# Five weight pieces of the mixing product split during the product before it, and one low part moved from GpSimd to VectorE

## The chip, the cores and the metric

The kernel runs on one core of a Trainium2 chip. The metric is the device time of one execution in microseconds (us). TensorE (PE) does the matrix products, VectorE (DVE) and ScalarE (ACT) the elementwise work, GpSimd (POOL) some of it too, and SyncE (SP) issues most of the DMAs that bring weights in.

## The reference, cut to what matters

The kernel computes one hybrid decoder block on x of 512 tokens by 1024 channels in float32:

```python
h = rmsnorm(x, norm1_g)
z = h @ w_in + b_in                     # split into glu, rx, rg, ga, gb
u = silu(layernorm(causal_conv(glu)))
y_a = u @ conv_w_out + conv_b_out       # "ya" in the kernel
y_b = (rg_lru(...) * gelu(rg)) @ lru_w_out
m = sigmoid(ga) * y_a + sigmoid(gb) * y_b
x = x + m @ w_mix_out                   # "mixing" (mx) in the kernel
h = rmsnorm(x, norm2_g)
x = x + (silu(h @ w1) * (h @ w3)) @ w2
return rmsnorm(x, norm_f_g)
```

## The kernel before, in words

Every matrix product in float32 is made of three products of split operands: each operand is cut into a high part, which ScalarE casts (`act.copy`, L128), and a low part, which is the rest (`sub`, L124), made by VectorE or by GpSimd. TensorE multiplies high by high, high by low and low by high.

The work runs in stages, in this order: z (in-projection), the convolution and the recurrence beside it, yb (L652), ya (`ya_group`, matmuls at L1393), mixing (`m7`, a `Sevenfold`, matmuls at L1316), the second norm with its transposes (`turn_half`, "th", L697) and the feed-forward layer (fr at L1567, then or). The products of ya and of mixing are done with seven block products in place of eight, so that some of their weights are sums of blocks: b11, b21, b22 are blocks of the weight matrix, and t1 to t4 are sums, which DMAs on GpSimd's queue add up in DRAM beforehand (tiles cot1 to cot4 and mxt1 to mxt4). ya is done in two groups, each with seven pieces (b11, b21, b22, t2, t1, t3, t4); 24 matmuls read each piece. Each piece of mixing's weights holds two blocks of 128x512.

All weights stream through one list of pieces ("chunks"). `wchunk` appends a piece to the list; SP's loads, ScalarE's casts and the low parts follow the order of that list. A piece is loaded into one of RAW = 8 raw tiles of 128x1024 (0.5 MB, tiles `raw_...`); a raw tile is free again when the low part of the piece eight places ahead of it has been made. The split goes either to one of HL = 5 tiles with room for both parts (`where="hl"`, tiles `hl_...`), which is free again when TensorE has read it; or, with `where="long"`, to four tiles of 128x512 from the pool of long-lived tiles: then it takes two casts and two subtractions of 128x512 in place of one each of 128x1024. `weights(key, ahead)` is what a product calls for its piece: it emits the splits up to `ahead` places beyond it. Before the change mixing's pieces stand behind all of ya's in the list, and all of them go to `hl` tiles.

Of mixing's pieces one, t4_0, has its low part made by GpSimd (`on_pool`), and one, b22_2, has its low part put off (`put_off`, done by `lows_put_off`). Then `mix_end` does the end of mixing: `second` is the last of the products with t2 and b22, `less` and `plus` subtract PSUM banks from, and add them to, the residual tiles x200 to x231 (x2, token tile t, half h), `scaled` and `scale` multiply by the reciprocal of the norm (tiles xs, L1469), `third` does the products with t4, and `turn_half` the transposes, whose outputs VectorE turns into h20l to h27l (L701). The feed-forward products start with fr<-h20h.

VectorE, ScalarE and SP take their instructions strictly in order. In the profile the tile names lack their digits: hl_cot is any of the pieces t1 to t4 of ya, hl_cob any of b11, b21, b22 of ya; hl_mxb and hl_mxt the same for mixing; mxr is any bank of mixing's products.

Of the kernel before, what the change touches and what calls it, by code (L numbers as in the profile page):

```python
# [8 lines left out]
F32 = mybir.dt.float32  # L9
# [4 lines left out]
P = 128  # L14
T = 512
# [11 lines left out]
ND = D // P  # L27
# [30 lines left out]
SUMS_OWN = 40  # L58
LO_BY_DVE = 8
MID_AT, MID_STEP = 38, 2  # L60


MIX_LATE_LAG, LATE_LAG = 1, 8
# [23 lines left out]
def tile_block(ctx, tc, a, out):  # L87
# [24 lines left out]
    vec, act, pe, pool_e = nc.vector, nc.scalar, nc.tensor, nc.gpsimd  # L112
# [5 lines left out]
    newest = {}  # L118
    put_off = []
# [3 lines left out]
    def sub(eng, o, x, y):  # L123
        return eng.tensor_tensor(out=o, in0=x, in1=y, op=ALU.subtract)  # L124

    def split_to(h, l, full, eng, copy=act.copy):

        newest["cast"] = copy(h, full)  # L128
        if eng is None:
            put_off.append((l, full, h.bitcast(F32)))  # L130
            return h, l
        last = sub(eng, l, full, h.bitcast(F32))
        newest["sub" if eng is pool_e else "low"] = last.ins
        return h, l

# [26 lines left out]
    def wchunk(key, src, kt, cols, where="hl", lo=pool_e, after=None):  # L162
        chunks.append((key, src, kt, cols, where, lo, after))
# [49 lines left out]
    def weights(key, ahead=AHEAD):  # L213
        i = next(i for i, c in enumerate(chunks) if c[0] == key)
        emit_to(i + 1 + ahead)
        newest["at"] = i
        return held.pop(key)
# [57 lines left out]
    def co_quarter(n, g):  # L275

        if n[0] == "t":
            assert "co" in sums_made
            return co_sums[n][:, g]
        k = CO_PAIRS[g][int(n[2]) - 1]  # L280
        c = 4 * (int(n[1]) - 1)
        return conv_out[:, c : c + 4, 2 * k * P : 2 * (k + 1) * P]

    CO_ORDER = [(n, g) for of in (("b11", "b21"), ("b22", "t2", "t1", "t3", "t4")) for g in range(2) for n in of]

    def co_chunk(n, g):

        def load(raw_t):
            newest["load"] = newest["any"] = nc.sync.dma_start(raw_t.rearrange("p (k n) -> p k n", k=4), co_quarter(n, g)).ins

        wchunk(f"co{n}_{g}", load, 4, 2 * P, lo=vec)

    for n, g in CO_ORDER:
        co_chunk(n, g)

    class Quartered:
        def __init__(self, name, w, kh, lo, parts=(), step=None, on_pool=(), put_off=()):


            self.name, self.w, self.kh = name, w, kh  # L300
            self.step = step or 1
            self.tile = lambda k, i: k + kh * i if self.step == 1 else 2 * k + i
            self.parts = {n: [None] * kh for n in parts}

            self.all_sums = {n: dram.tile([P, kh, T], F32, tag=f"{name}{n}", name=f"{name}{n}") for n in IN_PLACE if n not in parts}
            self.sums = {(n, k): v[:, k, :] for n, v in self.all_sums.items() for k in range(kh)}
            self.at = {}

            def quarter(n, k):
                if n[0] == "t":  # L310
                    assert self.name in sums_made
                    return self.sums[n, k]
                i, h = int(n[1]) - 1, int(n[2]) - 1
                return w[:, self.tile(k, i), h * T : (h + 1) * T]

            def chunk(key, of):
                def load(raw_t):
                    for i, q in enumerate(of):
                        nc.sync.dma_start(raw_t[:, i * T : (i + 1) * T], quarter(*q))

                for i, q in enumerate(of):
                    self.at[q] = (f"{name}{key}", i)
                wchunk(f"{name}{key}", load, len(of), T, lo=None if key in put_off else pool_e if key in on_pool else lo)


            for p_ in (("b11", "t1", "b21"), ("t2", "t3", "b22"), ("t4",)):
                p_ = [n for n in p_ if n not in parts]
                for k in range(kh):
                    if len(p_) % 2 and k % 2 == 0:
                        chunk(f"{p_[-1]}_{k}", [(p_[-1], i) for i in (k, k + 1) if i < kh])  # L330
                    if len(p_) > 1:
                        chunk(f"{p_[0]}_{k}", [(n, k) for n in p_[:2]])

        def order(self):
            return [self.tile(k, i) for k in range(self.kh) for i in range(2)]

        def get(self, k, *names, ahead=AHEAD):

            out = []
            for n in names:  # L340
                if n in self.parts:
                    out.append(self.parts[n][k])
                    continue
                key, i = self.at[n, k]
                if key not in self.loaded:
                    self.loaded[key] = weights(key, ahead)
                h, l = self.loaded[key]
                out.append((h[:, i, :], l[:, i, :]))
            return out

        loaded = {}

    mixq = Quartered("mx", a["w_mix_out"][0].rearrange("(k p) n -> p k n", p=P), ND // 2, vec, step=2, on_pool=("t4_0",), put_off=("b22_2",))
    w1 = a["ffn_w1"][0].rearrange("(k p) n -> p k n", p=P)
    w3 = a["ffn_w3"][0].rearrange("(k p) n -> p k n", p=P)

# [15 lines left out]
    def f_both(n, k, lo=vec):  # L372

        def load(raw_t):
            for i, w_ in enumerate((w1, w3)):
                if n[0] == "b":
                    src = f_quarter(n, k, w_, 0, 4)
                else:
                    c, e, _ = WHERE[n]
                    src = f_sums[k][:, i, int(c[1]), :].rearrange("p (k n) -> p k n", k=4)[:, :, e * P : (e + 1) * P]  # L380
                newest["any"] = nc.sync.dma_start(raw_t[:, i * T : (i + 1) * T].rearrange("p (k n) -> p k n", k=4), src).ins

        wchunk(f"f{n}_{k}", load, 8, P, lo=lo)
# [155 lines left out]
    for k in range(KF):  # L539
# [6 lines left out]
        else:  # L546
# [3 lines left out]
            if k + 1 in SEVEN:  # L550
                for j in BEGUN_LATER:
                    for n in ("b11", "b21", "t4"):
                        f_both(n, j)
    outq = Quartered("o", a["ffn_w2"][0].rearrange("(k p) n -> p k n", p=P), NF // 2, vec, step=2, on_pool=("t4_6",))
    x2_kept = [[dram.tile([P, T], F32, tag=f"x2k{t}{h}", name=f"x2k{t}{h}") for h in range(2)] for t in range(NT)]


# [105 lines left out]
    def rstd_mean(ss):  # L663
        vec.tensor_scalar(out=ss[:, 0:1], in0=ss[:, 0:1], scalar1=1.0 / D, scalar2=EPS, op0=ALU.mult, op1=ALU.add)
# [798 lines left out]
    def mix_end(second, plus, less, r1, r2, r7, third):  # L1463
        sc = [[longt(f"xs{t}{h}") for h in range(2)] for t in range(NT)]
        xs.extend(sc)
        begun = [rstd_begin(x2[t][0], sc[t][0], False) for t in range(2)]

        def scale(t, i, r):
            newest["scaled"] = vec.tensor_scalar(out=sc[t][i], in0=x2[t][i], scalar1=r, scalar2=None, op0=ALU.mult).ins  # L1469

        def scaled(t, h, some=(0, 1)):
            r = rstd_end(begun[t], x2[t][h], sc[t][h])
            for i in range(2):
                if i in some:
                    scale(t, i, r)
                nc.sync.dma_start(x2_kept[t][i][:, :], x2[t][i])
            return r


        with tc.manual_schedule(engines={ET.PE, ET.Activation, ET.DVE}):  # L1480
            second()
            less(0, 1, r1[0])
            plus(0, 1, r2[0])
            less(2, 1, r1[0])
            rstd_mean(begun[0][0])
            less(1, 1, r1[1])
            plus(1, 1, r2[1])
            rstd_mean(begun[1][0])
            less(3, 1, r1[1])

            rs = [scaled(t, 1, (0,)) for t in range(2)]
            for t in range(2):
                scale(t, 1, rs[t])

            for i in range(2):
                third(i, range(2))
            for q in range(2):
                turn_half("th", xs, "norm2_g", h2p, 0, [bank, bank2], range(4 * q, 4 * q + 4))
                for i in range(2):
                    third(i, [2 + q])  # L1500


            for c in range(ND):
                f_full.append(longt(f"hf{c}"))
                full(f_full[c][:, LO], c, LO)
            for i in range(2):
                less(2 + i, 1, r7[i])
                plus(2 + i, 0, r7[i])
            begun.extend(rstd_begin(x2[t][1], sc[t][1]) for t in (2, 3))
            emit_to(emitted[0] + 1)  # L1510
            for i in range(2):
                plus(2 + i, 0, r1[i])
            for t in (2, 3):
                scaled(t, 0)
# [81 lines left out]
    class Seven:  # L1596
# [14 lines left out]
        def copy(self):  # L1611
            self.c11 = shortt(f"c11_{self.k}")
            left_over(act.copy(self.c11, self.r1).ins)
# [248 lines left out]
```

## Time and profile before

| | |
|---|---|
| median of 3 runs | 786.73 us (786.65 to 786.78) |
| the profiled execution, its own time | 786.88 us |
| its span, first to last instruction | 785.1 us |
| TensorE busy | 775.5 us (99%) |
| VectorE busy | 677.2 us (86%) |
| ScalarE busy | 489.6 us (62%) |
| GpSimd busy | 292.4 us (37%) |
| granted TensorE clock | 1.0 |
| ya's matmuls | 364.81 to 405.13 us of the span |
| mixing's matmuls | 405.13 to 449.27 us, where the feed-forward layer starts |

Times of the trace are counted from the start of the span; the execution's own time is 1.78 us longer than the span. In the trace's rows stand the start, the duration and the instruction as out<-in with its shape; `[1.85 <-DVE stats L664]` says that the engine stood idle for 1.85 us before it and what ended that. Successive instructions of one engine overlap by a little, so what an instruction takes of the engine is the distance to the next start, not its duration.

### The profile page before, as it was taken

What the parts mean: (1) busy time and instruction counts of PE and PEld (TensorE: products, weight loads), DVE (VectorE), ACT (ScalarE), POOL (GpSimd) and SP (SyncE); (2) the same over time, 40 slices, a digit from 0 to 9 for tenths busy, and PEclk for the clock granted to TensorE, in tenths of its full rate; (3) what the DMA queues carried; (4) which work ended last, traced back from release to release, by engine and by line L of the source; (5) the groups of instructions that cost most, each with busy time, mean ns of one, the idle gap of its engine ahead of it and who ended that gap; (6) DMA issues with size and microseconds to landing.
All of it is one profiled execution on the core that took longest, in us unless ns stands there. A gap on an engine that the chain in (4) does not pass through costs nothing.

```text
span 785.1 us, 12621 instructions
## 1 busy us (share of the span) xinstructions
PE 775.5 (99%) x4469; PEld 684.1 (87%) x4469; DVE 677.2 (86%) x1028; ACT 489.6 (62%) x734; POOL 292.4 (37%) x240
## 2 busy tenths in 40 slices
PE   9999999999999999999999899999999999999997
PEld 9988788888888888888998698999999999888886
DVE  6389998899987997798799969779888889999957
ACT  8543678976786777566556576455554555666844
POOL 4365856577677973311101581312212220000001
PEclk9999999999999999999999999999999999999999
DMA  8827978796999996499977676998989794679522
GB/s 246 233 58 198 261 207 241 183 275 178 260 251 285 303 284 189 104 269 294 258 253 224 185 250 213 237 290 216 268 229 245 251 215 134 220 234 299 171 68 107
DMA packets 184753, 174.39 MB, mean 222 GB/s; under 512 B 14683, under 2 KB 145907, under 8 KB 184691
## 3 DMA queue, kind: packets, MB, share of 16 engines
q1 hardware_dynamic: 166034, 131.39, 57.0%
q0 software_dynamic: 18496, 41.95, 22.8%
q8 instruction: 35, 0.57, 0.3%
q10 hardware_dynamic: 160, 0.27, 0.1%
q14 instruction: 28, 0.22, 0.1%
HBM read 149.97 MB, written 50.33 MB: 255 GB/s over the span
## 4 chain that ended last, share of the span: by engine, by line
PE 89%; DVE 7%; DMA 2%; issue 1%; ACT 0%; SPq 0%; DVEq 0%
PE z L652 36%; PE fr L1567 25%; PE or L1316 13%; PE yb L652 7%; PE f L652 3%; PE g L1140 2%; PE ya L1393 1%; PE fr L1630 1%; DVE hl_mxb L124 1%; DVE hl_cot L124 1%; DVE hl_mxt L124 1%; DMA raw_mxb<-in_w_mix_out_dram 1%; DMA x<-in_x_dram 1%; DVE x L115 1%; DVE xs L1469 0%
## 5 line engine op out<-in xcount | busy, mean ns | idle before, releaser
L905 DVE SCALAR_TENSOR_TENSOR cv<-u,par,cv 128x507 f32<-128x507 f32 (+15 forms) x240 | 162.1, 733 | 4.2 <-ACT cv L901 3.4
L124 POOL TENSOR_TENSOR hl_in<-raw_in,hl_in 128x1024 fp32r<-128x1024 f32 (+1 forms) x52 | 124.4, 2412 | 66.4 <-ACT hl_in L128 57.3
L1567 PE MATMUL fr<-hs_0h,hl_ft 128*128 128x256 f32 x320 | 59.2, 283 | 0.0
L128 ACT CAST hl_in<-raw_in 128x1024 fp32r<-128x1024 f32 x50 | 51.4, 1047 | 1.4 <-DMA th<-tg 0.8
L1567 PEld LDWEIGHTS fr<-hs_0h,hl_ft 128*128 128x128 f32 x320 | 50.6, 192 | 0.0
L124 POOL TENSOR_TENSOR hl_ot<-raw_ot,hl_ot 128x1024 fp32r<-128x1024 f32 x1 | 2.4, 2417 | 121.3 <-ACT hl_ot L128 121.3
L494 POOL DMA_DIRECT2D ot<-in_ffn_w_dram x24 | 26.4, 1112 | 54.5 <-DVE hl_ft L124 33.3
L1567 PE MATMUL fr<-hs_0l,hl_ft 128*128 128x256 f32 x160 | 45.3, 283 | 0.0
L128 ACT CAST hl_fb<-raw_fb 128x1024 fp32r<-128x1024 f32 x30 | 31.3, 1046 | 21.1 <-PE fr L1567 10.9
L124 DVE TENSOR_TENSOR hl_fb<-raw_fb,hl_fb 128x1024 fp32r<-128x1024 f32 x27 | 33.2, 1228 | 10.4 <-ACT hl_fb L128 10.4
L652 PE MATMUL z<-h10h,hl_in 128*128 128x512 f32 (+1 forms) x108 | 41.1, 382 | 0.0
L652 PE MATMUL z<-h13h,hl_in 128*128 128x512 f32 (+1 forms) x108 | 40.8, 379 | 0.0
L652 PE MATMUL z<-h15h,hl_in 128*128 128x512 f32 (+1 forms) x108 | 40.8, 379 | 0.0
L652 PE MATMUL z<-h12h,hl_in 128*128 128x512 f32 (+1 forms) x108 | 40.8, 379 | 0.0
L652 PE MATMUL z<-h14h,hl_in 128*128 128x512 f32 (+1 forms) x108 | 40.8, 379 | 0.0
L652 PE MATMUL z<-h16h,hl_in 128*128 128x512 f32 (+1 forms) x108 | 40.8, 379 | 0.0
L652 PE MATMUL z<-h11h,hl_in 128*128 128x512 f32 (+1 forms) x108 | 40.8, 379 | 0.0
L652 PE MATMUL z<-h17h,hl_in 128*128 128x512 f32 (+1 forms) x108 | 40.8, 379 | 0.0
L128 ACT CAST hl_ft<-raw_fb 128x1024 fp32r<-128x1024 f32 x28 | 28.6, 1049 | 14.9 <-DVE raw_fb L115 11.8
L116 POOL TENSOR_TENSOR fws<-fws 128x256 f32<-128x256 f32 x44 | 36.9, 838 | 2.1
L128 ACT CAST hl_ob<-raw_ob 128x1024 fp32r<-128x1024 f32 (+1 forms) x23 | 23.3, 1015 | 21.1 <-PE or L1316 14.7
L124 DVE TENSOR_TENSOR hl_ft<-raw_fb,hl_ft 128x1024 fp32r<-128x1024 f32 x28 | 33.6, 1219 | 1.2 <-ACT hl_ft L128 1.2
(930 smaller groups left out, 2680.5 us busy)
## 6 DMA issues: line engine op xcount, KB each, us to landing
raw_in<-in_w_in_dram SPq DMA_DIRECT2D x51, 512.0 KB
raw_fb<-in_ffn_w_dram SPq DMA_DIRECT2D x74, 256.0 KB
ot<-in_ffn_w_dram POOLq DMA_DIRECT2D x30, 512.0 KB, 8.1
raw_ob<-in_ffn_w_dram SPq DMA_DIRECT2D x33, 256.0 KB
raw_ot<-ot SPq DMA_DIRECT2D x33, 256.0 KB
fws<-in_ffn_w_dram SPq DMA_DIRECT2D x12, 512.0 KB
cot<-in_conv_w_out_dram POOLq DMA_DIRECT2D x12, 512.0 KB, 8.8
mxt<-in_w_mix_out_dram POOLq DMA_DIRECT2D x12, 512.0 KB, 10.1
```

The lines of the kernel that those rows point to most:

```text
L115: add = lambda o, x, y: vec.tensor_tensor(out=o, in0=x, in1=y, op=ALU.add)
L116: plus_on = lambda eng, o, x, y: eng.tensor_tensor(out=o, in0=x, in1=y, op=ALU.add)
L124: return eng.tensor_tensor(out=o, in0=x, in1=y, op=ALU.subtract)
L128: newest["cast"] = copy(h, full)
L494: plus = lambda o, x: pool_e.dma_start(o, x, accum_op=ALU.add)
L652: pe.matmul(ps, l, r, start=i == 0, stop=i == n - 1)
L905: vec.scalar_tensor_tensor(out=acc[:, s:], in0=u[c][:, : T - s], scalar=dw(c, s), in1=acc[:, s:], op0=ALU.mult, op1=ALU.add)
L1140: pe.matmul(ps[:HB], head_chunk[0][:ROWS_G, g, h % 2, m, :], ext[h][m][:ROWS_G], start=m == 0, stop=m == 1)
L1316: pe.matmul(banks[i][:, cs], l_[:, ts], r_[:, cs], start=start and n == 0, stop=stop and n == 2, skip_group_check=again)
L1393: pe.matmul(ps[:, HALVES[i]], lw[:, c, cols], rx_, start=not (again or i or c or m), stop=bool(i and c == 3 and m == 2), skip_group_check= ...
L1567: pe.matmul(ps[:, HALVES[i]], lw[:, c, :], rx_, start=not (again or i or c or m), stop=bool(i and c == 3 and m == 2), skip_group_check=True,)
L1630: pe.matmul(self.r4[:, HALVES[i]], lw, rx_, start=not (i or c or m), stop=bool(i and c == 3 and m == 2), skip_group_check=True)
```

## The change

Five of mixing's pieces (b21_0, b11_0, b11_1, b21_2, b11_2) are put into the list among ya's, each behind the ya piece that the table `MX_EARLY` names, and go to long-lived tiles. The other nine pieces of mixing stay behind ya's. t4_0's low part is made by VectorE, and b22_2's is no longer put off. While `third` runs, a low part that is emitted is ordered behind the newest `scale`.

```diff
+MX_EARLY = {("b22", 0): ("b21_0",), ("t1", 0): ("b11_0",), ("t4", 0): ("b11_1",), ("b22", 1): ("b21_2",), ("t2", 1): ("b11_2",)}
...
-        last = sub(eng, l, full, h.bitcast(F32))
+        with tc.issue_after(newest["behind"]) if newest.get("behind") else nullcontext():
+            last = sub(eng, l, full, h.bitcast(F32))
...
-                wchunk(f"{name}{key}", load, len(of), T, lo=None if key in put_off else pool_e if key in on_pool else lo)
+                side = None if key in put_off else pool_e if key in on_pool else lo
+                self.plan[key] = lambda where: wchunk(f"{name}{key}", load, len(of), T, where=where, lo=side)
...
+        def planned(self, *keys):
+            for key in keys:
+                self.plan.pop(key)("long")
+            if not keys:
+                for key in list(self.plan):
+                    self.plan.pop(key)("hl")
...
-    mixq = Quartered("mx", ..., ND // 2, vec, step=2, on_pool=("t4_0",), put_off=("b22_2",))
+    mixq = Quartered("mx", ..., ND // 2, vec, step=2, on_pool=(), put_off=())
+    for n, g in CO_ORDER:
+        co_chunk(n, g)
+        if (n, g) in MX_EARLY:
+            mixq.planned(*MX_EARLY[n, g])
+    mixq.planned()
...
+            newest["behind"] = newest["scaled"]
             for i in range(2):
                 third(i, range(2))
+            newest["behind"] = None
```

On SP, the loads from ya's piece b22 of the first group to t1 of the second, before the change (cob and cot are ya's pieces, the last digit is the group):

```order
L289 DMA raw_cob22_0_3606<-in_conv_w_out_dram 128x4x256
L289 DMA raw_cot2_0_3639<-cot2_78 128x1024
L289 DMA raw_cot1_0_3672<-cot1_79 128x1024
L289 DMA raw_cot3_0_3705<-cot3_81 128x1024
L289 DMA raw_cot4_0_3770<-cot4_80 128x1024
L289 DMA raw_cob22_1_3799<-in_conv_w_out_dram 128x4x256
L289 DMA raw_cot2_1_3832<-cot2_78 128x1024
L289 DMA raw_cot1_1_3867<-cot1_79 128x1024
```

And now, on SP, the last part of the same stretch (raw_mxb21_0 stands ahead of these rows, behind raw_cob22_0; then come cot2_0 and cot1_0):

```order
L319 DMA raw_mxb11_0_3776<-in_w_mix_out_dram 128x512
L319 DMA raw_mxb11_0_3776<-mxt1_83 128x512
L291 DMA raw_cot3_0_3811<-cot3_81 128x1024
L291 DMA raw_cot4_0_3816<-cot4_80 128x1024
L319 DMA raw_mxb11_1_3849<-in_w_mix_out_dram 128x512
L319 DMA raw_mxb11_1_3849<-mxt1_83 128x512
L291 DMA raw_cob22_1_3890<-in_conv_w_out_dram 128x4x256
L319 DMA raw_mxb21_2_3895<-in_w_mix_out_dram 128x512 x2
L291 DMA raw_cot2_1_3949<-cot2_78 128x1024
L319 DMA raw_mxb11_2_4011<-in_w_mix_out_dram 128x512
L319 DMA raw_mxb11_2_4011<-mxt1_83 128x512
L291 DMA raw_cot1_1_4022<-cot1_79 128x1024
```

Five pieces of mixing now stand ahead of cot1_1 in SP's queue, where none stood; three pieces of ya's second group (cot1_1, cot3_1, cot4_1) are loaded behind them.

On ScalarE, the casts around the same piece, before:

```order
L128 CAST hl_cob22_1_3801<-raw_cob22_1_3799 128x1024
L1402 ACTIVATE q_0_3828<-ya1_0_3605,par_101 128x256 x2
L128 CAST hl_cot2_1_3834<-raw_cot2_1_3832 128x1024
L128 CAST hl_cot1_1_3869<-raw_cot1_1_3867 128x1024
L128 CAST hl_cot3_1_3917<-raw_cot3_1_3915 128x1024
L128 CAST mxus1h_3899<-sgb1_0_1371 128x512
```

And now:

```order
L129 CAST hl_cob22_1_3892<-raw_cob22_1_3890 128x1024
L129 CAST mxb11_1h1_3856<-raw_mxb11_1_3849 128x512
L129 CAST mxb21_2h0_3898<-raw_mxb21_2_3895 128x512
L1417 ACTIVATE q_0_3845<-ya1_0_3605,par_101 128x256 x2
L129 CAST mxb21_2h1_3902<-raw_mxb21_2_3895 128x512
L129 CAST hl_cot2_1_3951<-raw_cot2_1_3949 128x1024
L129 CAST hl_cot1_1_4024<-raw_cot1_1_4022 128x1024
L129 CAST hl_cot3_1_4053<-raw_cot3_1_4051 128x1024
L129 CAST mxus1h_3933<-sgb1_0_1371 128x512
```

The half casts of the early pieces stand between the casts of ya's; b11_2's halves (not in these rows) come later, on VectorE during mixing.

On VectorE, the end of mixing up to the first `less` of `mix_end` (x201<-x201,mxr10), before:

```order
L124 TENSOR_TENSOR hl_mxb22_2_4296<-raw_mxb22_2_4293,hl_mxb22_2_4296 128x1024
L124 TENSOR_TENSOR mxvb3l_4367<-sgb3_1_2660,mxvb3h_4366 128x512
L115 TENSOR_TENSOR x201_3961<-mxr50_4191,x201_3961 128x512
L115 TENSOR_TENSOR x221_3965<-mxr50_4191,x221_3965 128x512
L115 TENSOR_TENSOR x211_3963<-mxr51_4192,x211_3963 128x512
L115 TENSOR_TENSOR x231_3967<-mxr51_4192,x231_3967 128x512
L124 TENSOR_TENSOR hl_mxt4_2_4402<-raw_mxt4_2_4399,hl_mxt4_2_4402 128x1024
L124 TENSOR_TENSOR x201_3961<-x201_3961,mxr10_4187 128x512
```

And now:

```order
L125 TENSOR_TENSOR mxeb3l_4389<-mxe3_4222,mxeb3h_4388 128x512
L116 TENSOR_TENSOR x221_3999<-mxr50_4246,x221_3999 128x512
L125 TENSOR_TENSOR mxvb3l_4393<-sgb3_1_2660,mxvb3h_4392 128x512
L116 TENSOR_TENSOR x211_3997<-mxr51_4247,x211_3997 128x512
L116 TENSOR_TENSOR x231_4001<-mxr51_4247,x231_4001 128x512
L125 TENSOR_TENSOR hl_mxt4_0_4403<-raw_mxt4_0_4400,hl_mxt4_0_4403 128x1024
L125 TENSOR_TENSOR hl_mxt4_2_4427<-raw_mxt4_2_4424,hl_mxt4_2_4427 128x1024
L125 TENSOR_TENSOR x201_3995<-x201_3995,mxr10_4242 128x512
```

hl_mxt4_0's low part has come in ahead of hl_mxt4_2's, b22_2's has gone to an earlier place, and the adds of x201 to x231 stand among the late splits; from x201<-x201,mxr10 on VectorE's rows are the same. GpSimd's are the same but for the low part of hl_mxt4_0, which is gone. TensorE's matmuls are the same in number and, up to the tile names of the five pieces and three matmuls within mixing, in order.

More of the change, by code (lines that the diff above doesn't have):

```diff
@@ L291, in co_chunk @@
         wchunk(f"co{n}_{g}", load, 4, 2 * P, lo=vec)
-    for n, g in CO_ORDER:
-        co_chunk(n, g)
     class Quartered:
@@ L322, in chunk @@
                     self.at[q] = (f"{name}{key}", i)
-                wchunk(f"{name}{key}", load, len(of), T, lo=None if key in put_off else pool_e if key in on_pool else lo)
+                side = None if key in put_off else pool_e if key in on_pool else lo
+                self.plan[key] = lambda where: wchunk(f"{name}{key}", load, len(of), T, where=where, lo=side)
+            self.plan = {}
             for p_ in (("b11", "t1", "b21"), ("t2", "t3", "b22"), ("t4",)):
@@ L346, in get @@
                     self.loaded[key] = weights(key, ahead)
-                h, l = self.loaded[key]
-                out.append((h[:, i, :], l[:, i, :]))
+                of = self.loaded[key]
+                out.append(of[i] if isinstance(of, list) else tuple(v[:, i, :] for v in of))
             return out
         loaded = {}
-    mixq = Quartered("mx", a["w_mix_out"][0].rearrange("(k p) n -> p k n", p=P), ND // 2, vec, step=2, on_pool=("t4_0",), put_off=("b22_2",))
+    mixq = Quartered("mx", a["w_mix_out"][0].rearrange("(k p) n -> p k n", p=P), ND // 2, vec, step=2, on_pool=(), put_off=())
+    for n, g in CO_ORDER:
[3 more added lines that the diff above has]
+    mixq.planned()
     w1 = a["ffn_w1"][0].rearrange("(k p) n -> p k n", p=P)
@@ L554, in tile_block @@
     outq = Quartered("o", a["ffn_w2"][0].rearrange("(k p) n -> p k n", p=P), NF // 2, vec, step=2, on_pool=("t4_6",))
+    outq.planned()
     x2_kept = [[dram.tile([P, T], F32, tag=f"x2k{t}{h}", name=f"x2k{t}{h}") for h in range(2)] for t in range(NT)]
```

## The prediction

> **What bounds the kernel now.** I read the page's first lines, then what TensorE waits for, then each engine's timeline where it waits, then busy time in stretches of 10 us, then the DMA queues. First the page: its busy line for TensorE and the chain.
>
> ```profile
> span 785.1 us, 12621 instructions
> PE 775.5 (99%) x4469; PEld 684.1 (87%) x4469; DVE 677.2 (86%) x1028; ACT 489.6 (62%) x734; POOL 292.4 (37%) x240
> PE 89%; DVE 7%; DMA 2%; issue 1%; ACT 0%; SPq 0%; DVEq 0%
> ```
>
> TensorE is never idle for long, so a change that leaves its matmuls alone can win only where it waits. All its waits:
>
> ```profile
> PE mxr L1316 <- DVE stats L664: 1.8, 1, 1.8
> PE warm L621 <- DVE ones L613: 1.1, 1, 1.1
> PE th L697 <- DVE h20l L701: 0.6, 1, 0.6
> PE mxr L1316 <- DVE x L124: 0.4, 1, 0.4
> PE tx L713 <- DVE x L753: 0.2, 1, 0.2
> ```
>
> Those with mxr and th lie together at mixing's end, and from the feed-forward's first matmul on TensorE has no gap up to 775 us (325.70 busy of 325.70). So whatever moves that first matmul moves the end by as much.
>
> ```profile
> 434.17 0.39 PE L1316 MATMUL mxr<-hl_mxt,mxvb3l 128*128 128x512 f32 x1
> ...
> 439.80 0.73 PE L1316 MATMUL mxr<-hl_mxt,mxvb0h 128*128 128x512 f32 x2 [1.85 <-DVE stats L664]
> ...
> 441.91 0.73 PE L1316 MATMUL mxr<-hl_mxt,mxvb0h 128*128 128x512 f32 x2 [0.45 <-DVE x L124]
> ...
> 446.42 1.61 PE L697 MATMUL th<-ident,xs 128*128 128x128 f32 x8 [0.61 <-DVE h20l L701]
> ...
> 449.27 0.28 PE L1567 MATMUL fr<-h20h,hl_fb 128*128 128x256 f32 x1
> ```
>
> ```profile
> 449.30:775.00 325.70, 325.70 (x2237) 304.62 (x2236) 279.69 (x398) 184.42 (x272) 60.92 (x67) 1.00 0.78 218
> ```
>
> The waits sum to 1.85 + 0.45 + 0.61 = 2.91 us. Without them fr would start at 449.27 − 2.91 = 446.36: **2.9 us is all there is to win.** Who is late there is VectorE:
>
> ```profile
> 427.01 0.69 DVE L124 TENSOR_TENSOR mxvb2l<-sgb,mxvb2h 128x512 fp32r<-128x512 f32 x1 [0.28 <-ACT mxvb2h L128]
> 427.62 1.22 DVE L124 TENSOR_TENSOR hl_mxt<-raw_mxt,hl_mxt 128x1024 fp32r<-128x1024 f32 x1
> 428.76 0.68 DVE L124 TENSOR_TENSOR mxeb3l<-mxe,mxeb3h 128x512 fp32r<-128x512 f32 x1
> 429.36 1.22 DVE L124 TENSOR_TENSOR hl_mxb<-raw_mxb,hl_mxb 128x1024 fp32r<-128x1024 f32 x1
> 430.50 2.90 DVE L124 TENSOR_TENSOR mxvb3l<-sgb,mxvb3h 128x512 fp32r<-128x512 f32 x1
> 433.31 2.47 DVE L115 TENSOR_TENSOR x<-mxr,x 128x512 f32<-128x512 f32 x4
> 435.71 2.06 DVE L124 TENSOR_TENSOR hl_mxt<-raw_mxt,hl_mxt 128x1024 fp32r<-128x1024 f32 x1
> 437.68 0.67 DVE L124 TENSOR_TENSOR x<-x,mxr 128x512 f32<-128x512 f32 x1
> ```
>
> The last row is the first `less` of `mix_end`; call its start S0. From there VectorE's list stays as it is, so fr comes S0 + 449.27 − 437.68 = S0 + 11.59, unless TensorE is the later one: 446.36 plus what it waits earlier. By starts, a low part of 128x1024 costs VectorE 428.76 − 427.62 = 1.14, one of 128x512 0.60. Two rows are out of line: mxvb3l took 433.31 − 430.50 = 2.81 and the last hl_mxt (t4_2) 437.68 − 435.71 = 1.97, both while GpSimd made a low part:
>
> ```profile
> 429.71 3.13 POOL L124 TENSOR_TENSOR hl_mxt<-raw_mxt,hl_mxt 128x1024 fp32r<-128x1024 f32 x1 [48.93 <-DMA raw_fb<-in_ffn_w_dram]
> 434.28 2.40 POOL L124 TENSOR_TENSOR hl_fb<-raw_fb,hl_fb 128x1024 fp32r<-128x1024 f32 x1 [1.44 <-ACT hl_fb L128]
> ```
>
> VectorE's load by stretches (third pair of columns):
>
> ```profile
> 365.00:375.00 10.00, 10.00 (x85) 10.00 (x85) 6.91 (x10) 5.23 (x8) 1.89 (x3) 1.00 1.01 328
> 375.00:385.00 10.00, 10.00 (x86) 10.00 (x85) 6.39 (x7) 4.29 (x6) 1.55 (x2) 1.00 1.02 264
> 385.00:395.00 10.00, 10.00 (x86) 10.00 (x85) 9.96 (x16) 6.06 (x9) 0.00 (x0) 1.00 0.80 247
> ```
>
> It idles 3.09 us in the first and 3.61 in the second, and is full from 385 on. That is the room into which low parts can be brought.
>
> **The change part by part.** *Four pieces forward.* The lows of b21_0, b11_0, b11_1 and b21_2 leave the full stretch: −4 × 1.14 = −4.56 on VectorE. As halves they cost 8 × 0.60 = 4.80 ahead of it, where 6.70 us were idle; that covers them, and were the cover gone each would cost its 0.60 ahead of ya's next low part. ScalarE's ten half casts lie beside ya's matmuls, where it is busy 5.23 and 4.29 us of 10. The fifth, b11_2, is still made behind ya's pieces: 2 × 0.60 − 1.14 = +0.06.
>
> *t4_0 to VectorE.* +1.14. In return GpSimd's 3.13 us at 429.71 go, and with them mxvb3l's stretch, 2.81 − 0.60 = 2.21. GpSimd's hl_fb at 434.28 stays; by my order t4_2's low then lies outside of it, −(1.97 − 1.14) = −0.83. TensorE reads t4_0 only after S0, so its low is in time. b22_2's low costs the same 1.14 at its new place, and the `issue_after` gives GpSimd no new wait: both cost nothing, since no engine's list lengthens.
>
> *Order around cot1_1.* The add that makes c12 now stands behind hl_cot1_1's low part; counted from that low part this is +0.61 (386.56 − 385.95 below). The wait of 0.28 at 427.01 goes, as VectorE will be later than ScalarE there.
>
> ```profile
> 385.95 0.69 DVE L115 TENSOR_TENSOR c<-ya,q 128x512 f32<-128x512 f32 x1
> 386.56 1.21 DVE L124 TENSOR_TENSOR hl_cot<-raw_cot,hl_cot 128x1024 fp32r<-128x1024 f32 x1
> ```
>
> From cot1_1's low part to S0 VectorE needed 437.68 − 386.56 = 51.12 us. It will need 51.12 − 4.56 + 0.06 + 1.14 − 2.21 − 0.83 + 0.61 − 0.28 = **45.05 us**. Had that low part stayed at 386.56, S0 would come at 431.6 by VectorE, ahead of the product it subtracts (434.17 + 0.39 = 434.56).
>
> *But it will not stay there.* SP's five early pieces are 2.6 MB in front of cot1_1, and ScalarE's cast of it blocks everything behind, VectorE included. When does it land? At 330 to 332 us the DMAs were as good as empty (5 GB/s). From then on SP's queue (q1) moved:
>
> ```profile
> 330.00:332.00 2.00, 2.00 (x11) 1.65 (x10) 1.38 (x1) 1.86 (x3) 2.00 (x3) 1.00 0.16 5
> ```
>
> ```profile
> q1 hardware_dynamic: 4640, 8.37, 47.2%
> ```
>
> ```profile
> q1 hardware_dynamic: 5226, 9.44, 49.3%
> ```
>
> The first is 332 to 386 us, the second 332 to 390. In the new order cot1_1 is the 16th piece of SP's since 332 (cob21_0, cob11_1, cob21_1, cob22_0 and the rows of the order behind them): 16 × 0.524 = 8.39 MB. SP asks for it about when mxb11_0's lows are made, near 375, so the queue stays full and serves by position. The bytes alone reach 8.39 at 386.0. A piece is complete only with the last of 16 engines' shares, while later pieces are under way; if two further pieces (1.05 MB) have moved by then, it is 390 (9.44). For the other end: SP's slowest stretch, 360 to 375, gave 2.55 MB in 15 us (below), 0.170 per us. At that rate from 344 on (0.41 MB moved by then), the 8.39 are through at 344 + 7.98 / 0.170 = 390.9, and with the same 4 us of spread at about 395. I take 389.6, near the second row, because the queue is as full in the new order as there, and keep 386 to 395 for the range.
>
> ```profile
> q1 hardware_dynamic: 405, 0.41, 12.6%
> ```
>
> ```profile
> q1 hardware_dynamic: 1087, 2.55, 52.1%
> q0 software_dynamic: 690, 1.79, 49.8%
> ```
>
> ```profile
> q1 hardware_dynamic: 1525, 2.93, 57.3%
> q0 software_dynamic: 562, 1.11, 44.0%
> ```
>
> (332 to 344; 360 to 375; 375 to 390; q0 is GpSimd's queue.) Then the low part starts 1.1 us later, at 390.7, 4.1 us after its place of before, and by VectorE S0 = 390.7 + 45.05 = 435.8. Until mixing is under way VectorE runs some 4 us behind its old times, and TensorE meets it: the add that makes the second group's c12, which frees a PSUM bank, moves from 402.20 to about 407, and the adds into x200 and x210 likewise. Row by row I find about 2.2 us of such waits (0.65 near 408, the rest between 421 and 427); the bounds are 0 and 4.1.
>
> ```profile
> 402.20 0.68 DVE L115 TENSOR_TENSOR c<-ya,q 128x512 f32<-128x512 f32 x1
> ```
>
> So the product is ready at 434.56 + 2.2 = 436.8, which is S0, and fr comes at 436.8 + 11.6 = 448.4 by VectorE and at 446.36 + 2.2 = 448.56 by TensorE. The later counts: 449.27 − 448.56 = 0.71 us won. The profiled execution took 786.88, 1.78 over its span and 0.15 over the median of 786.73; 786.88 − 0.71 = 786.17, by the median **786.0**.
>
> **The rivals.** *The piece lands early.* If cot1_1 lands by 387, VectorE's 45.05 us end ahead of the product (388.1 + 45.05 = 433.2), S0 is 434.6 and all 2.9 us are won: 783.8. For it: bytes are there at 386.0. Against it: 9.44 MB by 390 with more asked for behind. Between 387 and 389.6 the win falls by 1 us per us.
>
> *The piece lands late* (the other side). Mechanism: SP's mixing pieces come in rows of 2 KB where cot's come in 4 KB, and share the engines with GpSimd's sums, so SP's queue gets less and cot1_1 comes later; ScalarE's cast of it blocks the casts behind it, then VectorE, then TensorE. Each us over 389.6 costs 1: the gain is gone at 390.3, over 0.2% is lost (1.57 us) from 391.9 on, and at 393 it is 789.4. For it: in the stretch from 360 to 375 q1 got 59% of the bytes. Against it: from 375 to 390, with rows of 2 KB, it got 73%. The Trainium skill, page "DMA: Bandwidth & Descriptors", section "Queues, rings and completion order", says that each DMA engine goes round the queues that have work a packet at a time, so that smaller packets would mean a smaller share; by that rule this rival would be the likeliest, at 789.4 or more. The two stretches do not bear it out, as GpSimd's queue had less to move in the second.
>
> *GpSimd holds t4_2's low after all.* If its hl_fb (2.40 from 434.28) starts just before that low part, VectorE waits until 436.7, S0 = 436.7 + 1.14 = 437.8, and nothing is won: 786.8. For it: mxvb3l, 2.81 in place of 0.60, ran until GpSimd ended. Against it: GpSimd waits for a cast that waits for TensorE, which is later too. The Trainium skill, page "SBUF — State Buffer", section "SBUF: two separate sides", calls this an exclusive lock that whoever starts first keeps for the whole instruction; the row at 430.50 agrees.
>
> **How the numbers follow.** Forecast 0.40; early 0.34; late 0.18; GpSimd's hold 0.08. A measurement here can tell about 0.2%, 1.57 us. Faster by more: the early case and 0.04 of the forecast (landing under 388.7), 0.38. Within: 0.34 of the forecast and the hold, 0.42. Slower by more: the late case and 0.02 of unknown waits, 0.20. The range runs from 783.4 (all waits won, 0.4 beyond for unknowns) to 788.8 (a landing at 392.4) and leaves out about 0.18.
>
> **What would show it.** Right: the first fr near 448.5; ScalarE's cast of hl_cot waits for a DMA near 385 to 390, VectorE idles some 4 us there; GpSimd has no low part near 430 and mxvb3l takes 0.68; new waits of TensorE in 405 to 430, and the 1.85 near 438 gone. Wrong: no idle of VectorE near 388 and fr near 446.3 (early), or TensorE waiting inside ya or over 3 us in mixing and fr after 450.8 (late), or a low part of over 2 us on VectorE near 435 (the hold).

## The result, and the profile after

The changed kernel takes 783.89 us (median of 7, 783.68 to 785.18) against 786.78 before (median of 7): a ratio of 0.9966, 95% interval 0.9954 to 0.9977. That is 2.9 us faster, inside the range of the prediction, and not its likeliest case (786.0) but its rival "the piece lands early" (783.8). The profiled execution took 783.79 us with a span of 782.0. One execution of ballast2, below, which took 956.92 us at a granted clock of 0.753, is in no ratio here.

All of TensorE's waits in the changed kernel, to be held against the five rows of before:

```profile
PE warm L636 <- DVE ones L628: 1.1, 1, 1.1
PE th L712 <- DVE h20l L716: 0.5, 1, 0.5
PE tx L728 <- DVE x L768: 0.3, 1, 0.3
```

Both waits with mxr are gone, and no new one has come up in ya or in mixing. The second block of transposes and the first feed-forward matmul on TensorE:

```profile
443.32 1.61 PE L712 MATMUL th<-ident,xs 128*128 128x128 f32 x8 [0.47 <-DVE h20l L716]
...
446.17 0.28 PE L1584 MATMUL fr<-h20h,hl_fb 128*128 128x256 f32 x1
```

fr starts at 446.17 in place of 449.27, 3.10 us earlier, and the span is 3.1 shorter (785.1 to 782.0): as before, nothing behind fr gives any of it back. Most of it lies between the last matmul ahead of the waits and the first block of transposes, before:

```profile
437.57 0.39 PE L1316 MATMUL mxr<-hl_mxt,mxeb3l 128*128 128x512 f32 x1
...
443.41 1.04 PE L697 MATMUL th<-ident,xs 128*128 128x128 f32 x8
```

and now:

```profile
437.49 0.39 PE L1331 MATMUL mxr<-hl_mxt,mxeb3l 128*128 128x512 f32 x1
...
440.44 1.03 PE L712 MATMUL th<-ident,xs 128*128 128x128 f32 x8
```

This stretch went from 5.84 to 2.95 us, 2.89 less, though the two waits listed in it were 1.85 + 0.45 = 2.30. On VectorE, the low part of cot1_1, then the last splits, adds and the first `less` (S0):

```profile
386.28 1.22 DVE L125 TENSOR_TENSOR hl_cot<-raw_cot,hl_cot 128x1024 fp32r<-128x1024 f32 x1
...
427.79 0.68 DVE L125 TENSOR_TENSOR mxvb3l<-sgb,mxvb3h 128x512 fp32r<-128x512 f32 x1
428.39 1.28 DVE L116 TENSOR_TENSOR x<-mxr,x 128x512 f32<-128x512 f32 x2
429.59 2.48 DVE L125 TENSOR_TENSOR hl_mxt<-raw_mxt,hl_mxt 128x1024 fp32r<-128x1024 f32 x2
434.52 0.69 DVE L125 TENSOR_TENSOR x<-x,mxr 128x512 f32<-128x512 f32 x1 [2.45 <-PE mxr L1331]
```

mxvb3l takes 0.68 in place of 2.90, both lows of t4 together 2.48, and VectorE now waits 2.45 us for TensorE ahead of S0: it had been the late one, and is the early one. The 4 us of idle time near 388 that the forecast expected is not there. ScalarE's cast of cot1_1 shows why; it waits for a matmul to free its tile, and not for a DMA:

```profile
385.09 1.05 ACT L129 CAST hl_cot<-raw_cot 128x1024 fp32r<-128x1024 f32 x1 [0.59 <-PE ya L1408]
```

The room on VectorE has been used (third pair of columns; 6.91 and 6.39 before):

```profile
365.00:375.00 10.00, 10.00 (x86) 10.00 (x85) 9.08 (x14) 6.80 (x12) 2.08 (x3) 1.00 1.04 370
375.00:385.00 10.00, 10.00 (x85) 10.00 (x85) 8.90 (x12) 6.82 (x10) 0.80 (x1) 1.00 1.07 267
```

GpSimd's next two low parts start 0.66 and 3.10 us earlier (434.28 and 443.30 before):

```profile
433.62 2.40 POOL L125 TENSOR_TENSOR hl_fb<-raw_fb,hl_fb 128x1024 fp32r<-128x1024 f32 x1 [57.83 <-ACT hl_fb L129]
440.20 2.38 POOL L125 TENSOR_TENSOR hl_fb<-raw_fb,hl_fb 128x1024 fp32r<-128x1024 f32 x1 [4.18 <-ACT hl_fb L129]
```

The first starts while VectorE waits for TensorE and holds nobody: VectorE's first `less`, at 434.52 and beside it, takes 0.69 (0.67 before). The second still meets the fourth scaling, which leaves the 0.47 at the transposes.

### The profile page after: what moved, and what is told of

It reads as the page before. It is cut to its first block, busy times and chain, and to the rows that moved or that the text cites. A ratio compares the mean times of both kernels' runs of the same rounds, so it can differ in the third digit from the quotient of the medians.

```text
span 782.0 us, 12628 instructions
## 1 busy us (share of the span) xinstructions
PE 774.8 (99%) x4469; PEld 684.1 (87%) x4469; DVE 677.2 (87%) x1034; ACT 490.4 (63%) x739; POOL 289.7 (37%) x239
## 4 chain that ended last, share of the span: by engine, by line
PE 97%; DVE 1%; DMA 1%; ACT 0%; issue 0%; SPq 0%; DVEq 0%
PE z L667 36%; PE fr L1584 25%; PE or L1331 13%; PE yb L667 7%; PE ya L1408 5%; PE mxr L1331 4%; PE f L667 3%; PE g L1155 2%; PE fr L1647 1%; DMA x<-in_x_dram 1%; DVE xs L1484 1%; PE tx L728 0%; PE th L712 0%; PE z L785 0%; DVE x L125 0%; DVE x L116 0%
```

## The experiments

The room theory: what counts is VectorE's load between cot1_1's low part and S0, whatever makes it smaller, and S0 is the later one of VectorE's end and TensorE's product. Its rival, the lock theory: GpSimd's low part at 429.7 was all that held the end up.

### pool_only: the second half of the change alone

```diff
-    mixq = Quartered("mx", ..., step=2, on_pool=("t4_0",), put_off=("b22_2",))
+    mixq = Quartered("mx", ..., step=2, on_pool=(), put_off=())
```

(on the kernel before)

> The kernel before, with the second half of the change alone: t4_0's low part on VectorE, b22_2's not put off, no piece forward. Room theory (the win is VectorE's load ahead of S0, whatever makes it smaller): 51.12 + 1.14 - 2.21 - 0.83 = 49.22 us from cot1_1's low part at 386.56, S0 at 435.8, fr at 447.4, about 784.9; TensorE still waits some 0.5 to 1.0 us at its first product with t4. Lock theory (GpSimd's low part at 429.7 is all that held the end up): S0 at 434.6 and 783.9, like the whole change.

Measured: 787.16 us, ratio 1.0003 (0.9994 to 1.0011): nothing won. Both theories fail as stated. VectorE and GpSimd at the end of mixing:

```profile
433.40 4.55 DVE L124 TENSOR_TENSOR hl_mxt<-raw_mxt,hl_mxt 128x1024 fp32r<-128x1024 f32 x2
437.88 0.67 DVE L124 TENSOR_TENSOR x<-x,mxr 128x512 f32<-128x512 f32 x1
```

```profile
434.03 2.84 POOL L124 TENSOR_TENSOR hl_fb<-raw_fb,hl_fb 128x1024 fp32r<-128x1024 f32 x1 [55.28 <-ACT hl_fb L128]
```

The two lows of t4 take 4.48 to the next start in place of 2.28. They run into GpSimd's next low part, so S0 is 437.88, where the load alone gives 437.88 − 2.20 = 435.7 as expected. This is the prediction's third rival, "GpSimd holds t4_2's low", in a kernel where VectorE's second low part would start at 433.40 + 1.14 = 434.54, 0.5 us too late to be ahead of GpSimd's.

### pool_only_late: the same, with GpSimd's next low part moved away

```diff
-                last = get(kh - 1, "b22", "t2", "t3", ahead=AHEAD - 1)
+                last = get(kh - 1, "b22", "t2", "t3", ahead=AHEAD - 2)
...
-                third(i, range(2))
+                third(i, range(2), ahead=2)
```

(`third` hands `ahead` on to `get`)

> pool_only with one thing more: the piece fb11_1 of the feed-forward layer, whose low part GpSimd makes at 434.03, is split one step later (the last of mixing's products with t2 and b22 fetches one piece less ahead, the first ones with t4 two ahead in place of three). If GpSimd's low part held VectorE's two lows of t4 in pool_only (4.48 us in place of 2.28): the pair takes 2.28, S0 comes at 435.7 as the sum had it, and the time is 784.9 to 785.3. If something else made pool_only slow: 787.1 again.

Measured: 790.50 us, ratio 1.0056 (1.0043 to 1.0070). At mixing's end it is as expected:

```profile
433.49 2.35 DVE L124 TENSOR_TENSOR hl_mxt<-raw_mxt,hl_mxt 128x1024 fp32r<-128x1024 f32 x2
435.76 0.68 DVE L124 TENSOR_TENSOR x<-x,mxr 128x512 f32<-128x512 f32 x1
```

```profile
447.34 0.28 PE L1567 MATMUL fr<-h20h,hl_fb 128*128 128x256 f32 x1
...
459.76 0.55 PE L697 MATMUL th<-ident,xs 128*128 128x128 f32 x3 [2.08 <-DVE xs L1469]
```

The hold is gone, S0 is 435.76 (435.7 was expected) and fr starts at 447.34, 1.93 us earlier than before. Then it is lost again: 2.08 at the transposes of the other two token tiles, and in the output product a wait of 2.6:

```profile
PE or L1316 <- DVE hl_ot L124: 2.6, 1, 2.6
```

So the cause of pool_only's loss is shown, and a second thing with it: an earlier fr is worth its time only while the order behind it stays.

### early_only: the first half alone

```diff
-    mixq = Quartered("mx", ..., step=2, on_pool=(), put_off=())
+    mixq = Quartered("mx", ..., step=2, on_pool=("t4_0",), put_off=("b22_2",))
```

(on the changed kernel)

> The changed kernel with t4_0's low part back on GpSimd and b22_2's put off again; five pieces forward as in the change. Room theory: VectorE ended 2.45 us ahead of the product in the changed kernel (432.07); it loses 1.14 of load and gets up to 3.0 us of holding by GpSimd back, so it ends at 431 to 434, still ahead of 434.5, and the time is that of the whole change, 783.9. Lock theory: 786 or more, as before.

Measured: median 783.82 us, ratio 0.9971 (0.9961 to 0.9982), as the room theory had it. But three of the 12 executions took 786.4 to 788.1, and the profiled one (786.42) is one of them. ScalarE and VectorE there:

```profile
387.96 1.05 ACT L129 CAST hl_cot<-raw_cot 128x1024 fp32r<-128x1024 f32 x1 [3.30 <-DMA raw_cot<-cot]
```

```profile
429.94 2.76 DVE L125 TENSOR_TENSOR mxvb3l<-sgb,mxvb3h 128x512 fp32r<-128x512 f32 x1
...
434.42 2.80 DVE L125 TENSOR_TENSOR hl_mxt<-raw_mxt,hl_mxt 128x1024 fp32r<-128x1024 f32 x1
437.15 0.68 DVE L125 TENSOR_TENSOR x<-x,mxr 128x512 f32<-128x512 f32 x1
```

In this execution cot1_1 came at 387.96, 2.9 us later than in the profiled one of the whole change, and VectorE, that much later, met both of GpSimd's low parts (2.76 in place of 0.68, 2.80 in place of 1.22). So pieces forward alone can win it all, but without t4_0's move they do not when the piece is late, as in this execution; the two other slow ones have no profile.

### one_early and three_early: how many pieces it takes

```diff
-MX_EARLY = {("b22", 0): ("b21_0",), ("t1", 0): ("b11_0",), ("t4", 0): ("b11_1",), ("b22", 1): ("b21_2",), ("t2", 1): ("b11_2",)}
+MX_EARLY = {("b22", 0): ("b21_0",)}
```

> The changed kernel with one piece (b21_0) forward in place of five. Room theory: 1.90 us by the low part on VectorE and 1.14 by the piece, 3.04 in all, S0 at 434.6 to 434.7, 783.9 to 784.1, and VectorE's wait of 2.45 us ahead of S0 shrinks to nearly nothing. A theory by which each piece brings its share of the gain: 784.9 - 0.2 = 784.7.

Measured: 784.07 us (783.80 to 784.24), ratio 0.9963 (0.9950 to 0.9976).

```profile
432.73 2.35 DVE L125 TENSOR_TENSOR hl_mxt<-raw_mxt,hl_mxt 128x1024 fp32r<-128x1024 f32 x2
435.00 0.68 DVE L125 TENSOR_TENSOR x<-x,mxr 128x512 f32<-128x512 f32 x1
```

One piece brings the two lows of t4 out of the way of GpSimd's next one, which starts at 434.55, when the second of them is under way. S0 is 435.00 (434.6 to 434.7 was expected), with VectorE's wait gone as expected; the gain is not shared out over the pieces.

Three pieces (b21_0, b11_0 and b11_1, the table cut after its third entry):

> The changed kernel with three pieces forward (b21_0, b11_0, b11_1) in place of five. cot1_1 then has 1.05 MB less ahead of it and lands some 4 us earlier; VectorE's slack ahead of S0 shrinks from 2.45 by 1.14 to about 1.3. Room theory: nothing lost, 783.8 to 783.9, and no execution above 784.5, since a late landing of cot1_1 no longer meets anything. If all five pieces are needed: 785.0.

Measured: 783.64 us (783.59 to 783.80), ratio 0.9959 (0.9946 to 0.9971), with no execution above 783.8.

```profile
434.63 0.69 DVE L125 TENSOR_TENSOR x<-x,mxr 128x512 f32<-128x512 f32 x1 [1.69 <-PE mxr L1331]
```

### ballast2: the landing that the prediction had assumed

```diff
...
+            if (n, g) == ("t1", 1):
+                for i in range(2):
+                    with tc.issue_after(newest["load"]):
+                        newest["load"] = nc.sync.dma_start(ballast[i], a["w_in"][0][i * P : (i + 1) * P, :D]).ins
...
```

(ahead of cot1_1's load, on the changed kernel)

> The changed kernel with two transfers of 0.5 MB more on SP's queue straight ahead of cot1_1's load (128 rows of 4 KB of w_in, copied to DRAM tiles that nobody reads). At 0.223 MB per us (3.34 MB in 15 us) cot1_1 lands some 4.7 us later, at 389.5, the landing that the prediction had assumed. If the rest of the prediction's sum is right: VectorE idles about 4 us near 386 to 390, 2.45 of it is covered by its slack ahead of S0, TensorE waits some 2 us in mixing, and the time is 785.8. If a late piece is hidden in some way that the sum doesn't have: 783.9.

Measured: five executions from 788.65 to 789.26 us and three from 785.28 to 786.47, these last near the 785.8 that was expected; the ratio is 1.0011 (0.9999 to 1.0024). The profiled execution (789.17) is one of the five and tells why they are slower. ScalarE, VectorE and TensorE in it:

```profile
392.63 1.05 ACT L129 CAST hl_cot<-raw_cot 128x1024 fp32r<-128x1024 f32 x1 [8.11 <-DMA raw_cot<-cot]
```

```profile
393.71 1.22 DVE L125 TENSOR_TENSOR hl_cot<-raw_cot,hl_cot 128x1024 fp32r<-128x1024 f32 x1 [7.33 <-ACT hl_cot L129]
...
436.88 2.34 DVE L125 TENSOR_TENSOR hl_mxt<-raw_mxt,hl_mxt 128x1024 fp32r<-128x1024 f32 x2
439.88 0.69 DVE L125 TENSOR_TENSOR x<-x,mxr 128x512 f32<-128x512 f32 x1 [0.65 <-PE mxr L1337]
```

```profile
451.52 0.28 PE L1590 MATMUL fr<-h20h,hl_fb 128*128 128x256 f32 x1
```

The piece came at 392.63, not at 389.5. That is 7.5 us later than in the change's profiled execution, but the 1 MB is not all of it: SP's first load of ya stands at 327.60 here, as in early_only (327.60) and no_hold (327.81, below), and at 325.80 in the change. Against those two, whose casts stand at 387.96 and 387.26, the piece is 4.7 to 5.4 us later, near the 4.7 that was worked out. With that landing the prediction's own law (fr at 448.56 for 389.6, and 1 us per us behind it) gives 451.6; measured are 451.52. The price is as it was told, in this one execution. The way is so in part: TensorE waits 1.32 for the add that makes c12 (0.65 near 408 was told) and 0.41 near 428 to 429, but also 2.04 inside ya for ScalarE's q, which the forecast's sum did not have and which was the prediction's sign of a late piece.

### cot_halves: does the size of the rows matter?

On the kernel before, each load of ya's t1 to t4 as two transfers:

```diff
...
+            for k in (0, 2) if n[0] == "t" else (0,):
+                m = 2 if n[0] == "t" else 4
+                newest["load"] = newest["any"] = nc.sync.dma_start(rv[:, k : k + m], src[:, k : k + m]).ins
```

> The kernel before with each load of ya's t1 to t4 as two transfers of 0.25 MB (two of the four blocks each, rows of 2 KB in place of 4 KB). It tells whether rows of 2 KB alone make SP's queue move more: if so, SP's queue moves 8.7 to 9.1 MB from 332 to 386 us, as with pieces forward, in place of 8.37; if it is that more is asked for earlier, 8.3 to 8.4 as before. The time is that of before, 786.8, either way.

Measured: 786.86 us, ratio 0.9999 (0.9989 to 1.0009). SP's queue, first in the changed kernel from 332 to 386 us, then in this one from 334 to 388 (this execution stood 2.1 us later at SP's first load of ya, 327.94 in place of 325.87):

```profile
q1 hardware_dynamic: 5116, 9.05, 50.3%
```

```profile
q1 hardware_dynamic: 5679, 8.17, 49.2%
```

More packets, and no more bytes: 8.17 MB (8.3 to 8.4 was expected) beside 8.37 before and 9.05 after. So rows of 2 KB alone do not make the queue move more.

### no_hold and three_fb_vec: the wait that is left

no_hold, on the changed kernel: the piece fb21_1 is split one step later.

```diff
-                third(i, range(2))
+                third(i, range(2), ahead=2)
```

(`third` hands `ahead` on to `get`, as in pool_only_late)

> The changed kernel with the piece fb21_1, whose low part GpSimd starts at 440.20 just as VectorE comes to its fourth scaling (3.47 us for the three from 439.40 in place of 1.20), split one step later, behind the first transposes. If GpSimd's low part is what holds that scaling: the wait of 0.47 at the transposes goes and the time is 783.4. If the low part of fb21_1 then comes too late for the feed-forward's second product: a wait of TensorE there and 784 or more.

Measured: 787.81 us, ratio 1.0010 (1.0001 to 1.0019). VectorE's three scalings and TensorE:

```profile
439.52 1.28 DVE L1484 TENSOR_SCALAR xs<-x,stats 128x512 f32<-128x512 f32 x3
...
455.52 3.26 DVE L1484 TENSOR_SCALAR xs<-x,stats 128x512 f32<-128x512 f32 x2
```

```profile
445.37 0.39 PE L1584 MATMUL fr<-h20h,hl_fb 128*128 128x256 f32 x1 [0.15 <-DVE h24l L716]
...
458.83 0.55 PE L712 MATMUL th<-ident,xs 128*128 128x128 f32 x3 [3.00 <-DVE xs L1484]
```

```profile
456.16 2.33 POOL L125 TENSOR_TENSOR hl_ft<-raw_ft,hl_ft 128x1024 fp32r<-128x1024 f32 x1 [0.18 <-ACT hl_ft L129]
```

The hold is gone (1.28 in place of 3.47) and fr starts 0.8 earlier. But another of GpSimd's low parts now meets the scalings of the other token tiles, and TensorE waits 3.00 for them. Neither theory had this: the hold has moved. From fr to the end this execution takes 340.7 us where the changed kernel's takes 335.8. Of these 4.9 us the wait is 3.0. From 1.1 us behind it the granted clock (third figure from the end) is 0.50:

```profile
460.00:463.30 3.30, 3.30 (x17) 3.30 (x17) 1.61 (x4) 1.88 (x4) 3.07 (x3) 0.50 0.52 129
```

Half of these 3.3 us, 1.7, is lost by estimate, and with it all but 0.2 of the 4.9 is accounted for.

three_fb_vec, on three_early: fb21_1's low part on VectorE, behind the scalings.

```diff
-            f_both(n, k, vec if (n, k) == ("b21", 2) else pool_e)
+            f_both(n, k, vec if n == "b21" else pool_e)
```

> three_early with fb21_1's low part made by VectorE, behind the fourth scaling (which the change's issue_after now orders), in place of GpSimd. VectorE then does three scalings in 1.2 us in place of 3.4 and the low part in 1.14, so h20l starts about 1 us earlier, TensorE's wait of 0.41 at the transposes goes, and the time is 783.2. If, as in no_hold, GpSimd's later low parts then meet VectorE's scalings of the other two token tiles near 455: a new wait of TensorE near 459 and 785 or more.

Measured: 782.77 us (782.66 to 783.03), ratio 0.9946 (0.9933 to 0.9960): faster than both kernels, 1.1 us ahead of the change, which took 783.89 beside it. VectorE and TensorE:

```profile
439.42 1.28 DVE L1484 TENSOR_SCALAR xs<-x,stats 128x512 f32<-128x512 f32 x3
440.62 1.22 DVE L125 TENSOR_TENSOR hl_fb<-raw_fb,hl_fb 128x1024 fp32r<-128x1024 f32 x1
441.75 0.48 DVE L716 SCALAR_TENSOR_TENSOR h20l<-th,par,h20h 128x256 fp32r<-128x256 f32 x1
```

```profile
442.72 1.18 PE L712 MATMUL th<-ident,xs 128*128 128x128 f32 x8
...
445.12 0.28 PE L1584 MATMUL fr<-h20h,hl_fb 128*128 128x256 f32 x1
```

No wait of TensorE is left in mixing, and nothing comes back later. It won more than the wait of 0.41 that was expected: the eight transposes take 1.18 in place of 1.61, so that row, 1.61 before and in the change, had 0.43 of pauses inside it.

### after_again: one more landing

> The changed kernel once more, beside three_fb_vec on the same chip: 783.9, with single executions of 784.5 to 785.5 where cot1_1 lands some 3 us later than in the profiled execution; a second profile of it shows one more landing of cot1_1, expected between 384.8 and 388.0.

Measured: 783.89 us (783.75 to 785.04), ratio 0.9963 (0.9950 to 0.9975). ScalarE's cast in this execution:

```profile
385.86 1.05 ACT L129 CAST hl_cot<-raw_cot 128x1024 fp32r<-128x1024 f32 x1 [1.18 <-DMA raw_cot<-cot]
```

The landing lies in the range that was expected. The one execution of 785.04 has no profile, so what made it slow is not shown.

## Why the prediction was right and wrong

**What bounds.** Right in kind. The waits were VectorE's lateness, and an fr 3.1 us earlier ends the span 3.1 earlier. "2.9 us is all there is to win" was too little: the 1.85 and 0.45 went, of the 0.61 0.47 stayed, and three_fb_vec put fr at 445.12, 4.15 ahead of before. The floor was made from waits that a view lists, and a wait can cost more than its listed length: the 1.85 and 0.45 gave back 2.89, by starts, and 0.43 more stood as pauses within a row of eight transposes.

**VectorE's load.** Right to 0.5 us. 45.05 us were summed from cot1_1's low part to S0; in the changed kernel it is 429.59 + 2 × 1.14 − 386.28 = 45.6 to the end of the lows, and 436.88 + 2 × 1.14 − 393.71 = 45.45 in ballast2. The term for GpSimd's low part needs a condition, though. pool_only shows that −2.21 − 0.83 is not what it is worth by itself: VectorE then runs into GpSimd's next low part and gets 2.20 back. The pieces forward carry it past; one is enough.

**The landing of cot1_1.** This is the step that failed: "I take 389.6, near the second row, because the queue is as full in the new order as there". In the profiled execution the piece was there by 385.09. Its request was placed rightly (near 375; it was 375.67), but not what follows from it. SP's queue moved 9.05 MB by 386 and not 8.37. And at 385.09 the queue had moved 8.80 MB since 332, so that at most 0.41 MB of later pieces had gone before cot1_1 was complete, and not 1.05; in early_only, the latest landing in this order of loads, it was 9.22 MB by 387.9, 0.83 of them later pieces. What goes with the first is that SP asked earlier. Its 16th piece was asked for at 379.17 before and at 375.67 now:

```profile
379.17 0.33 SPq L319 DMA_DIRECT2D raw_mxb<-in_w_mix_out_dram  x1
379.55 0.42 SPq L319 DMA_DIRECT2D raw_mxb<-mxt  x1
```

```profile
375.67 3.53 SPq L291 DMA_DIRECT2D raw_cot<-cot  x3
```

A raw tile is asked for when a low part has freed it, so low parts in VectorE's idle time let SP ask sooner. That this is the cause is argued from the two rows and from cot_halves, which speaks against the row size; it was not tried by itself. A mean DMA share of 1.01 and 1.02 from 365 to 385 (next to last figure of the stretches) did not mean that no more could be moved: it is 1.04 and 1.07 in the changed kernel, with more bytes.

Nor is there one landing. In the same order of SP's loads up to it, the cast came at 385.09 and 385.86 in the change, at 387.26 in no_hold and at 387.96 in early_only. The two late ones go with a later start of SP's loads for ya, 327.81 and 327.60 in place of 325.80 and 325.97, while ya's first matmul stayed between 364.74 and 364.91. The change and early_only:

```profile
325.80 16.73 SPq L291 DMA_DIRECT2D raw_cob<-in_conv_w_out_dram  x5
```

```profile
327.60 17.31 SPq L291 DMA_DIRECT2D raw_cob<-in_conv_w_out_dram  x5
```

Why SP starts at the one time or the other is not shown. A single number out of a wide range was taken as the likeliest. The point from which it matters, 387, was near: with a landing of 387.26 in no_hold TensorE has no wait with mxr and VectorE still waits 0.77 ahead of S0, so it lies at about 388, an estimate from these two numbers.

**The rivals.** "Early" is what happened: 783.8 told, 783.89 measured. The bytes came even sooner than its 386.0. That the price fits to 0.1 us is partly luck: of the 2.91 that it counted as won 0.47 stayed, and 0.59 that no wait listed was won beside them. "Late" is real as a mechanism: ballast2 agrees with its law to 0.1 us. What the prediction drew for it from a page is not borne out in size. The Trainium skill, page "DMA: Bandwidth & Descriptors", section "Queues, rings and completion order", has the engines go round the queues a packet at a time; the prediction took rows of 2 KB for smaller packets, and so for a smaller share. In cot_halves the packets that the profile counts in SP's queue went from 4640 to 5679 and the bytes from 8.37 to 8.17 MB, 2% less; in the changed kernel the bytes went up. A packet of the page holds several descriptors, and no run here shows how rows fill one, so the rule itself is not tested. "GpSimd holds t4_2's low" did not happen in the changed kernel, where that low part was over at 432.07 and GpSimd began at 433.62, and decided pool_only. The Trainium skill, page "SBUF — State Buffer", section "SBUF: two separate sides", calls it an exclusive lock for a whole instruction; the 4.55 for two low parts that alone take 2.35 agrees.

**The small edits.** b22_2's place and the half casts cost nothing that shows. No run has the `issue_after` alone taken away, so what it costs or brings in the change is not shown; in three_fb_vec the low part that it orders, then VectorE's, starts at 440.62, right behind the fourth scaling.

## What to carry to other kernels

Where an engine on the path is held by another engine's long instructions, count not only the one that is removed: ask which the next one is, and whether the work, now earlier, comes past it or runs into it; one half of this change alone won nothing (787.16) and the other half in most executions all of it (783.82), which the sum of their terms did not say. For a load in a bounded set of buffers, work out when it is asked for (who frees its buffer) before asking how fast it is served, and give its landing a range of some us, with the point from which it matters; compare landings between executions only where the queue started at the same time. And an earlier start carries to the end only while the order behind it is kept: two kernels that started the feed-forward 1.9 and 3.9 us earlier ended later than before.

## What the hardware showed that was not expected

One piece of 0.5 MB in the same order of loads was taken up at 385.09, 385.86, 387.26 or 387.96 us from one execution to the next, while the casts on ScalarE ahead of it kept their times within 0.2 us; the later two are those in which SP's loads for ya started 1.6 to 2.0 us later. With 1.05 MB more ahead it came 4.7 to 5.4 us later than with the same start of those loads, 0.20 to 0.22 MB per us, which is about the 0.22 that the queue moves over 15 us.

A wait of TensorE cost more than its length. In no_hold the granted clock was 0.50 from 460.0 to 463.3, 1.1 us behind the wait of 3.00, and matmuls of 128x256 started 0.21 us apart in place of 0.12. The same 0.50 stands in pool_only from 441.4 to 444.6, behind a wait of 2.14, and in cot_halves from 443.3 to 446.5, behind one of 1.86; before, with one of 1.85, the clock stayed at 1.00. In pool_only it cost nothing that shows, since fr came 11.60 us after S0, as before (11.59).

VectorE's fourth scaling lost to GpSimd's low part in every kernel that had that order, by margins that the rows hardly show (440.20 on GpSimd, where 439.40 + 2 × 0.4 = 440.2 on VectorE). The two keep this distance when both move, to 0.06 us in ten executions; what ties them is not shown.
